# Long convolutions of a hybrid encoder layer: transforms in three rounded passes instead of one fp32 pass, with their matrices streamed in by group

## The chip, the cores and the metric

The kernel runs on one core of one Trainium2 chip. The metric is the device time of one execution in microseconds (us), as the median of the runs shown; smaller is better. The profile was taken of one execution of the same program. Engines are named as in the profile: PE multiplies matrices (PEld loads its weights), DVE is the vector engine, ACT the scalar engine, POOL the GpSimd engine, SP the queue that issues most transfers.

## The reference, cut to what matters

Two sequences of 1024 tokens by 1024 features go through one encoder layer. The layer has a projection, a "hyena" mixer with two long convolutions in a row, a windowed attention, gates, an output projection and a gated feed-forward. The change is in the long convolutions alone:

```python
def bidir_fftconv(u, h_fwd, h_bwd):
    L = u.shape[1]
    k = jnp.concatenate([h_fwd, jnp.zeros_like(h_fwd[:1]), h_bwd[:0:-1]], axis=0)
    k_f = jnp.fft.rfft(k, n=2 * L, axis=0)
    u_f = jnp.fft.rfft(u, n=2 * L, axis=1)
    return jnp.fft.irfft(u_f * k_f[None], n=2 * L, axis=1)[:, :L]

    for o, gate in enumerate((x1, x2)):
        z = gate.astype(jnp.float32) * (bidir_fftconv(z, filt[:, 0, o], filt[:, 1, o])
                                        + hyena_bias[o].astype(jnp.float32) * z)
```

The filters `filt` come from a small network and are the same for both sequences.

## The kernel before

**Products.** Nearly all large products are done in "three rounded passes": an fp32 operand is split into a rounded half `hi` (type fp32r) and the rest `lo`, and hi·hi, hi·lo and lo·hi are accumulated. ACT writes `hi` by a copy that rounds, DVE writes `lo` by a subtraction (`part`, `split`). The transforms of the long convolutions are the exception: they multiply plain fp32 operands.

**Transforms.** A transform of length 2048 is done in eight groups g = 0, 4, 2, 6 (the even half, part 0) and 1, 7, 3, 5 (the odd half, part 1). DVE forms the group's inputs A (128x512) by butterflies (`fwd_butterfly`), and PE multiplies them by a small matrix of the group (`dft`): one product of 512 columns and two of 256, or four of 256 for g = 0. `mats` loads all matrices of a direction once, into a tile of their own for each group, through SP. `conv` takes each group's result X (a PSUM bank of tag `sa`, of which there are two), loads the filter's spectrum K (three buffers), multiplies on DVE (t2, t1, then Y in two halves), transforms back on PE into `sb` or `sc`, and ACT copies the result to B. After the four groups of a half, `inv_even` or `inv_odd` joins them on DVE. The second of the two convolutions (`fm`) takes Y as the weights and the matrix as the moving operand, four products of 256 columns.

**Amount.** `filters` transforms the filters: 2 orders x 2 channel halves x 8 groups = 32 forward transforms. `hyena(s)` does, for each sequence s, 2 channel halves x 2 convolutions x 8 groups: 32 forward and 32 inverse transforms. "A half" below is the four groups between two butterflies, forward and inverse: hyena has eight halves for each sequence.

**Order.** In `main`, a chain of side work (filters, hyena(0), attention(0), hyena(1), attention(1)) is mixed with the projections (the "main" work) at fixed rates: each `yield` tells the cost that is counted. This gives the program's order and priorities. From them the framework fixes, at build time, the order of the instructions on each engine; on the chip every engine runs its list in order and waits where an operand is missing. The main work beside hyena(0) is the gates of sequence 0 (`proj_gates`: DVE scales each product, `ge<-mm,rf`) and then `next_rows`, which splits the normalised rows of sequence 1 (ACT `hh`, DVE `hl`) and starts its projection (`proj_u`); beside hyena(1) it is `proj_qkv` and `proj_gates` of sequence 1, whose results ACT copies out. The weights of the main work come through SP and are split by ACT (`whi`) and DVE (`wlo`).

Of the kernel before, what the change touches and what calls it, by code (L numbers as in the profile page):

```python
# [11 lines left out]
F32 = mybir.dt.float32  # L12
# [30 lines left out]
TB = 3  # L43
PA, YI, KB = 4, 2, 3
AB, YB = 3, 2
RATES = (1.0, 0.85, 1.0, 1.0, 1.1, 1.22, 1.3, 0.3)
# [3 lines left out]
PLACE = {"B11": 0, "B21": 1, "B22": 2, "T1": 3, "T3": 4, "T4": 5, "T2": 6}  # L50
PLAIN = (0, 1, 10)


def shape_constants():
# [30 lines left out]

    c["dft_f"], c["dft_i"], c["dft_f0"], c["dft_i0"] = (np.ascontiguousarray(x.astype(f32)) for x in (fwd, inv, fwd0, inv0))
    bands = 16
# [129 lines left out]
class Kern:  # L217
# [13 lines left out]
    def filters(self):  # L231
        nc, a, tc = self.nc, self.a, self.tc
        self.kd = [[self.dr.tile([P, 8, 3, CH], F32, name=f"kd{o}{h}") for h in range(2)] for o in range(2)]
        with tc.tile_pool(name="fl", bufs=1, side="right", reuse_waits="tile") as pool:
# [34 lines left out]
            with tc.tile_pool(name="fc", bufs=1, side="right", reuse_waits="tile") as cpool:  # L269
                mf = self.mats(cpool, "dft_f")  # L270
                for o in range(2):
# [6 lines left out]
                    for h in range(2):  # L278
# [16 lines left out]
                        for part, op in ((0, ALU.add), (1, ALU.subtract)):  # L295
                            nc.vector.tensor_tensor(sx, kt[:, 0:8], kt[:, 8:16], op)
                            for g, X in self.spectrum(cpool, sx, part, mf):
                                ks = cpool.tile([P, 3, CH], F32, tag="ks", name="ks", bufs=2)
                                nc.scalar.copy(ks[:, 0:2], X)
                                if g == 0:  # L300
                                    nc.scalar.copy(ks[:, 2], X[:, 0])
                                    nc.vector.tensor_copy(ks[0:1, 2], X[0:1, 1])
                                    nc.vector.memset(ks[0:1, 1], 0.0)
                                n = 3 if g == 0 else 2
                                nc.sync.dma_start(self.kd[o][h][:, g, :n], ks[:, :n])
                                yield 3
# [29 lines left out]

    def mats(self, pool, name):

        m = {}
        for g in (0, 4, 2, 6, 1, 7, 3, 5):  # L340
            m[g] = pool.tile([P, 4 if g == 0 else 3, P], F32, tag=f"{name}{g}", name=f"{name}{g}", bufs=1)
            self.nc.sync.dma_start(m[g], self.a[name + "0"][0] if g == 0 else self.a[name][g - 1])
        return m

    def spectrum(self, pool, x, part, mf):
        nc = self.nc
        Ag = {}

        def A(g):
            Ag[g] = pool.tile([P, 2, CH], F32, tag="A", name="A", bufs=AB)  # L350
            return Ag[g]

        def tmp(tag, n):
            return pool.tile([P, n, CH], F32, tag=tag, name=tag, bufs=1)

        for g in fwd_butterfly(nc, x, A, tmp, part):
            X = self.psm().rearrange("p (i c) -> p i c", i=2)
            self.dft(X, mf[g], Ag[g], g)
            yield g, X

    def dft(self, out, m, x, g):
        mm = self.nc.tensor.matmul
        if g:
            mm(out, m[:, 1], x, start=True, stop=False)
            mm(out[:, 0], m[:, 0], x[:, 1], start=False, stop=False)
            mm(out[:, 1], m[:, 2], x[:, 0], start=False, stop=True)
            return
        for o in range(2):
            for i in range(2):
                q = (1, 0, 2, 3)[2 * o + i]  # L370
                self.nc.tensor.matmul(out[:, o], m[:, q], x[:, i], start=(i == 0), stop=(i == 1))

    def conv(self, pool, z, o, h, fm, mf, mi):
        nc = self.nc
# [7 lines left out]
        for part in range(2):  # L382
            cnt = 0
            for g, X in self.spectrum(pool, z, part, mf):
                K = pool.tile([P, 2, CH], F32, tag="K", name="K", bufs=KB)
                nc.sync.dma_start(K, self.kd[o][h][:, g, 0:2])
                Kd = K[:, 0]
                if g == 0:
                    Kd = pool.tile([P, CH], F32, tag="Kd", name="Kd", bufs=1)
                    nc.sync.dma_start(Kd, self.kd[o][h][:, 0, 2])  # L390
                t1 = pool.tile([P, 2, CH], F32, tag="t1", name="t1", bufs=YB)
                t2 = pool.tile([P, 2, CH], F32, tag="t2", name="t2", bufs=1)
                nc.vector.tensor_tensor(t2, X, bc(K[:, 1], 2, 1), ALU.mult)
                if g == 0:
                    nc.vector.tensor_tensor(t1[:, 0], X[:, 0], K[:, 0], ALU.mult)
                    nc.vector.tensor_tensor(t1[:, 1], X[:, 1], Kd, ALU.mult)
                else:
                    nc.vector.tensor_tensor(t1, X, bc(K[:, 0], 2, 1), ALU.mult)
                Y = t1
                nc.vector.tensor_tensor(Y[:, 0], t1[:, 0], t2[:, 1], ALU.subtract)  # L400
                nc.vector.tensor_tensor(Y[:, 1], t2[:, 0], t1[:, 1], ALU.add)
                ps = self.psm("sb" if g % 4 < 2 else "sc")
                B[g] = pool.tile([P, 2, CH], F32, tag="B", name="B", bufs=4)
                if not fm:
                    X2 = ps.rearrange("p (i c) -> p i c", i=2)
                    self.dft(X2, mi[g], Y, g)
                    nc.scalar.copy(B[g], X2)
                else:
                    X2 = ps.rearrange("p (t c) -> p t c", t=2)
                    for t in range(2):  # L410
                        s = slice(P * t, P * t + P)
                        for i in range(2):
                            q = slice(1, 3) if i == 0 else slice(0, 4, 3) if g == 0 else slice(0, 2)
                            nc.tensor.matmul(X2[:, t], Y[:, i, s], mi[g][:, q], start=(i == 0), stop=(i == 1))
                    nc.scalar.copy(B[g].rearrange("p c (t n) -> p t c n", t=2), ps.rearrange("p (t c n) -> p t c n", t=2, c=2))
                cnt += 1
                yield 4.5
# [5 lines left out]
    def hyena(self, s):  # L423
        nc, tc = self.nc, self.tc
        with tc.tile_pool(name="cv", bufs=1, side="right", reuse_waits="tile") as pool:
            mf, mi = self.mats(pool, "dft_f"), self.mats(pool, "dft_i")
            for h in range(2):
# [3 lines left out]
                nc.sync.dma_start(x1, self.x1t[s][:, :, h])  # L431
                for y in self.conv(pool, z, 0, h, False, mf, mi):
                    if isinstance(y, float):
                        yield y
# [3 lines left out]
                yield 2.5  # L438
                for yf in self.conv(pool, y, 1, h, True, mf, mi):
                    if isinstance(yf, float):  # L440
                        yield yf
# [126 lines left out]
    def spread_dma(self, pool, r):  # L568
# [3 lines left out]
        nc.tensor.transpose(pt[:NB, :P], r, self.ident)  # L572
        row = pool.tile([NB, P], F32, tag="row", name="row", bufs=1)
        nc.scalar.copy(row, pt[:NB, :P])
# [857 lines left out]
```

## Time and profile before

| what | value |
|---|---|
| median of 3 runs | 2963.36 us (2956.32 to 2964.63) |
| the profiled execution: its time, its span | 2963.17 us, 2961.4 us |
| filters' transforms | about 148 to 371 us of the span |
| hyena(0) | about 371 to 633 us |
| attention(0) beside the projection of sequence 1 | about 633 to 880 us |
| hyena(1) | about 880 to 1150 us |
| DVE TENSOR_TENSOR of 128x512 | 0.69 us each |
| ACT CAST of 128x512 to fp32r | 0.62 us each |

A row of the grouped view reads: line, engine, operation, out<-in, shape, xcount, then busy time and the mean ns of one, then the idle time before. A row of the timeline reads: start and duration in us, engine, line, operation. A matmul's duration contains the drain of its pipeline, which lies beside the next one; the distance from start to start ("pitch") is what it costs in a row of its kind. The same holds, less strongly, for DVE.

### The profile page before, as it was taken

The numbers are of one execution on the slowest core, as the hardware profiler recorded it, in microseconds if no ns is written. First come the engines' busy times: TensorE is split into PE (matmuls) and PEld (weight loads), VectorE is DVE, ScalarE is ACT, GpSimd is POOL, SyncE is SP. The second block draws the span as 40 slices with busy tenths as digits, with TensorE's granted clock in tenths as the row PEclk, the third lists the DMA queues.
The fourth block names the chain that finished last, engine by engine and source line by source line (L and its number), as shares of the span: only waits on it lengthen the run. The fifth ranks groups of instructions, "written<-read, shape, count | busy, mean of one in ns | idle before, by whom it ended". The sixth has DMA issues, their size and how long they took to land.

```text
span 2961.4 us, 35810 instructions
## 1 busy us (share of the span) xinstructions
PE 2905.0 (98%) x13386; PEld 2349.2 (79%) x13386; DVE 2068.7 (70%) x3361; ACT 1151.4 (39%) x1870; POOL 74.9 (3%) x146
## 2 busy tenths in 40 slices
PE   8999999999999999999999999999999999999998
PEld 6788777778887777777777788888887888888887
DVE  6675698787858755888587667776555767766565
ACT  5322211148841112887464434444111434443122
POOL 0000000000000000000000000000122000001100
PEclk9999999999999999999999999999999999999999
DMA  5444763242253323544776345556666334447641
GB/s 172 143 136 144 263 212 132 100 151 69 77 180 95 141 96 113 159 153 148 221 230 201 121 156 202 205 206 243 262 249 248 136 121 156 157 156 290 260 156 69
DMA packets 202427, 498.29 MB, mean 168 GB/s; under 512 B 19623, under 2 KB 68427, under 8 KB 202253
## 3 DMA queue, kind: packets, MB, share of 16 engines
q1 hardware_dynamic: 182093, 422.60, 41.9%
q0 software_dynamic: 20160, 73.41, 6.3%
q8 instruction: 105, 1.72, 0.2%
q14 instruction: 69, 0.57, 0.1%
HBM read 342.30 MB, written 153.63 MB: 167 GB/s over the span
## 4 chain that ended last, share of the span: by engine, by line
PE 66%; DVE 6%; DMA 4%; ACT 3%; issue 1%; SPq 0%; DVEq 0%; ACTq 0%
PE mm L517 5%; PE mm L518 5%; PE mm L519 5%; PE mm L1003 4%; PE mm L1004 4%; PE mm L1005 4%; PE sa L1003 3%; PE sa L1004 3%; PE sa L1005 3%; PE mm L1200 1%; PE mm L1201 1%; PE mm L1202 1%; PE sb L1003 1%; PE sb L1004 1%; PE sb L1005 1%; PE sc L1003 1%
## 5 line engine op out<-in xcount | busy, mean ns | idle before, releaser
L325 ACT CAST whi<-raw 128x1024 fp32r<-128x1024 f32 (+1 forms) x270 | 264.3, 979 | 627.0 <-PE mm L518 277.6
L326 DVE TENSOR_TENSOR wlo<-raw,whi 128x1024 fp32r<-128x1024 f32 (+1 forms) x270 | 306.3, 1134 | 208.1 <-ACT whi L325 197.7
L518 PE MATMUL mm<-hl,whi 128*128 128x512 f32 x824 | 330.9, 402 | 0.0
L517 PE MATMUL mm<-hh,whi 128*128 128x512 f32 x824 | 330.6, 401 | 0.0
L519 PE MATMUL mm<-hh,wlo 128*128 128x512 f32 x824 | 328.2, 398 | 0.0
L325 ACT CAST whi<-s 128x1024 fp32r<-128x1024 f32 x104 | 109.1, 1049 | 254.8 <-PE mm L1004 57.2
L1003 PE MATMUL mm<-r,whi 128*128 128x512 f32 x528 | 207.9, 394 | 0.2 <-ACT r L325 0.2
L1004 PE MATMUL mm<-r,whi 128*128 128x512 f32 x528 | 206.9, 392 | 0.8 <-DVE r L326 0.8
L1005 PE MATMUL mm<-r,wlo 128*128 128x512 f32 x528 | 206.6, 391 | 0.0
L517 PEld LDWEIGHTS mm<-hh,whi 128*128 128x128 f32 x824 | 155.8, 189 | 30.7 <-issue 0.7
L519 PEld LDWEIGHTS mm<-hh,wlo 128*128 128x128 f32 x824 | 155.6, 189 | 30.4 <-issue 0.5
L518 PEld LDWEIGHTS mm<-hl,whi 128*128 128x128 f32 x824 | 155.8, 189 | 30.2 <-issue 0.5
L1003 PE MATMUL sa<-r,whi 128*128 128x512 f32 x352 | 139.1, 395 | 4.6 <-ACT whi L325 4.6
L1004 PE MATMUL sa<-r,whi 128*128 128x512 f32 x352 | 138.3, 393 | 0.0
L1005 PE MATMUL sa<-r,wlo 128*128 128x512 f32 x352 | 138.2, 393 | 0.0
L326 DVE TENSOR_TENSOR wlo<-s,whi 128x1024 fp32r<-128x1024 f32 x104 | 127.0, 1222 | 13.8 <-ACT whi L325 12.3
L982 POOL DMA_DIRECT2D r<-comb x112 | 59.4, 530 | 2683.9 <-PE mm L1005 2061.1
L1004 PEld LDWEIGHTS mm<-r,whi 128*128 128x128 f32 x528 | 99.1, 188 | 23.1 <-DVE r L326 1.1
L1003 PEld LDWEIGHTS mm<-r,whi 128*128 128x128 f32 x528 | 99.2, 188 | 22.6 <-ACT r L325 0.3
L1005 PEld LDWEIGHTS mm<-r,wlo 128*128 128x128 f32 x528 | 99.1, 188 | 22.7
L725 PE MATMUL mm<-whi,hh 128*128 128x256 f32 x384 | 110.2, 287 | 0.0
L726 PE MATMUL mm<-wlo,hh 128*128 128x256 f32 x384 | 109.3, 285 | 0.0
(471 smaller groups left out, 7036.1 us busy)
## 6 DMA issues: line engine op xcount, KB each, us to landing
r<-comb POOLq DMA_DIRECT2D x112, 512.0 KB, 9.6
comb<-stage SPq DMA_DIRECT2D x48, 1024.0 KB, 5.1
raw<-in_w_fg SPq DMA_DIRECT2D x44, 512.0 KB, 5.6
raw<-in_w_fu SPq DMA_DIRECT2D x44, 512.0 KB, 3.5
raw<-in_w_g SPq DMA_DIRECT2D x32, 512.0 KB, 4.4
gt<-ge SPq DMA_DIRECT2D x32, 512.0 KB, 5.2
K<-kd SPq DMA_DIRECT2D x64, 256.0 KB, 3.5
raw<-in_w_up SPq DMA_DIRECT2D x32, 512.0 KB, 4.4
```

Of the source, the lines that this page charges most:

```text
L325: self.nc.scalar.copy(hi, src)
L326: self.nc.vector.tensor_tensor(lo, src, hi.bitcast(F32), ALU.subtract)
L517: mm(ps, hi[:, k], xh[:, s], start=(i == 0), stop=False)
L518: mm(ps, hi[:, k], xl[:, s], start=False, stop=False)
L519: mm(ps, lo[:, k], xh[:, s], start=False, stop=(i == n - 1))
L725: nc.tensor.matmul(ps[:, q], xh[:, t], wh, start=(i == 0), stop=False)
L726: nc.tensor.matmul(ps[:, q], xh[:, t], wl, start=False, stop=False)
L982: self.nc.gpsimd.dma_start(t.bitcast(F32), src[q][PLACE[name]])
L1003: mm(ps, hi[:, k], xh, start=(first and k == 0), stop=False, skip_group_check=not first)
L1004: mm(ps, hi[:, k], xl, start=False, stop=False, skip_group_check=not first)
L1005: mm(ps, lo[:, k], xh, start=False, stop=(k == n - 1), skip_group_check=not first)
L1200: mm(ps, hi[:, w], xh, start=(first and q == 0), stop=False, skip_group_check=not first)
```

## The change

A transform's matrix is split on the host into `hi` and `lo` (`halves`), and the table holds both. `mat` loads one group's pair when its turn comes, into one of two buffers of that direction, by a transfer that POOL issues and that turns fp32 into fp32r; `mats` is gone. The inputs A and the products Y are split by ACT and DVE (`split`, two buffers each), and each product is done in three passes. To make room, K has two buffers in place of three, A two in place of three, t1 one in place of two, t2 shares the butterfly's `t`, and a small row tile uses another tile's tag.

```diff
-PA, YI, KB = 4, 2, 3
-AB, YB = 3, 2
+PA, YI, KB = 4, 2, 2
+AB, YB = 2, 1
+MB = 2
+def halves(x):
+    x = np.ascontiguousarray(x.astype(np.float32))
+    i = x.view(np.int32)
+    hi = ((i + 0x7FF + ((i >> 12) & 1)) & ~0xFFF).astype(np.int32).view(np.float32)
+    return np.ascontiguousarray(np.stack([hi, x - hi], axis=2))
...
-    c["dft_f"], c["dft_i"], c["dft_f0"], c["dft_i0"] = (np.ascontiguousarray(x.astype(f32)) for x in (fwd, inv, fwd0, inv0))
+    c["dft_f"], c["dft_i"], c["dft_f0"], c["dft_i0"] = (halves(x) for x in (fwd, inv, fwd0, inv0))
...
-    def mats(self, pool, name):
-        m = {}
-        for g in (0, 4, 2, 6, 1, 7, 3, 5):
-            m[g] = pool.tile([P, 4 if g == 0 else 3, P], F32, tag=f"{name}{g}", name=f"{name}{g}", bufs=1)
-            self.nc.sync.dma_start(m[g], self.a[name + "0"][0] if g == 0 else self.a[name][g - 1])
-        return m
+    def mat(self, pool, name, g):
+        src = self.a[name + "0"][0] if g == 0 else self.a[name][g - 1]
+        n = int(np.prod(src.shape[1:]))
+        t = pool.tile([P, 8 * P], F32R, tag=name, name=name, bufs=MB)
+        t = t[:, :n].rearrange("p (e q c) -> p e q c", e=2, q=src.shape[2])
+        self.nc.gpsimd.dma_start(t, src)
+        return t
...
         for g in fwd_butterfly(nc, x, A, tmp, part):
+            m = self.mat(pool, "dft_f", g)
             X = self.psm().rearrange("p (i c) -> p i c", i=2)
-            self.dft(X, mf[g], Ag[g], g)
+            self.dft(X, m, self.split(pool, Ag[g], [P, 2, CH], "A"), g)
             yield g, X
...
+        passes = [(m[:, e], x[f]) for e, f in ((0, 0), (0, 1), (1, 0))]
         if g:
-            mm(out, m[:, 1], x, start=True, stop=False)
-            mm(out[:, 0], m[:, 0], x[:, 1], start=False, stop=False)
-            mm(out[:, 1], m[:, 2], x[:, 0], start=False, stop=True)
+            for n, (w, v) in enumerate(passes):
+                mm(out, w[:, 1], v, start=(n == 0), stop=False)
+            for n, (w, v) in enumerate(passes):
+                mm(out[:, 0], w[:, 0], v[:, 1], start=False, stop=False)
+                mm(out[:, 1], w[:, 2], v[:, 0], start=False, stop=(n == 2))
             return
...
-                t2 = pool.tile([P, 2, CH], F32, tag="t2", name="t2", bufs=1)
+                t2 = tmp("t", 2)
...
+                Y = self.split(pool, Y, [P, 2, CH], "Y")
+                mi = self.mat(pool, "dft_i", g)
...
-                            nc.tensor.matmul(X2[:, t], Y[:, i, s], mi[g][:, q], start=(i == 0), stop=(i == 1))
+                            for n, (e, f) in enumerate(((0, 0), (0, 1), (1, 0))):
+                                nc.tensor.matmul(X2[:, t], Y[f][:, i, s], mi[:, e, q], start=(i == 0 and n == 0), stop=(i == 1 and n == 2))
```

The order shows two places. The first is PE in hyena(0), from the end of the second forward transform of an odd half to the start of the third (`mm` is the gates' product of main work, `hh`, `hl` its moving operands; `Ah`, `Al` the split inputs of the transform). Of the change:

```order
L378 MATMUL sa<-Ah,dft_f 128x256
L379 MATMUL sa<-Ah,dft_f 128x256
L534 MATMUL mm<-hl_306,whi 128x512
L535 MATMUL mm<-hh_305,wlo 128x512
L533 MATMUL mm<-hh_329,whi 128x512
L534 MATMUL mm<-hl_330,whi 128x512
L535 MATMUL mm<-hh_329,wlo 128x512
L533 MATMUL mm<-hh_165,whi 128x512
L534 MATMUL mm<-hl_166,whi 128x512
L535 MATMUL mm<-hh_165,wlo 128x512
L533 MATMUL mm<-hh_185,whi 128x512
L376 MATMUL sa<-Ah,dft_f 128x512
```

Between the second transform and the third stand nine products of main work; the third needs a matrix whose buffer the first one has held.

The second place is DVE in the fifth half of hyena(0) (the first convolution of the second channel half), at the groups 2 and 6. Before:

```order
L393 TENSOR_TENSOR t_3794<-sa,K 128x512
L398 TENSOR_TENSOR t_3793<-sa,K 128x512
L178 TENSOR_TENSOR sd<-t,B 128x512
L400 TENSOR_TENSOR t_3793<-t_3793,t_3794 128x256
L401 TENSOR_TENSOR t_3793<-t_3794,t_3793 128x256
L744 TENSOR_TENSOR ge<-mm,rf 128x512
L393 TENSOR_TENSOR t_3814<-sa,K 128x512
L398 TENSOR_TENSOR t_3813<-sa,K 128x512
```

And of the change, at the same groups (`Yl` and `Al` are the new `lo` halves, `hl` the rows of sequence 1):

```order
L407 TENSOR_TENSOR t<-sa,K 128x512
L342 TENSOR_TENSOR Yl<-t_4496,Yh 128x512
L342 TENSOR_TENSOR Al<-A,Ah 128x512
L412 TENSOR_TENSOR t_4607<-sa,K 128x512
L334 TENSOR_TENSOR hl_5646<-xin,hh_5645 128x512
L414 TENSOR_TENSOR t_4607<-t_4607,t 128x256
L415 TENSOR_TENSOR t_4607<-t,t_4607 128x256
L334 TENSOR_TENSOR hl_5654<-xin,hh_5653 128x512
L407 TENSOR_TENSOR t<-sa,K 128x512
L342 TENSOR_TENSOR Yl<-t_4607,Yh 128x512
L334 TENSOR_TENSOR hl_5654<-xin,hh_5653 128x512
L412 TENSOR_TENSOR t_4651<-sa,K 128x512
```

The `lo` halves stand one instruction behind the value that they split, and the rows of sequence 1 (`hl`), which had come in the last half of hyena(0) and behind it, stand here, three halves ahead of that.

More of the change, by code (lines that the diff above doesn't have):

```diff
@@ L269, in filters @@
             with tc.tile_pool(name="fc", bufs=1, side="right", reuse_waits="tile") as cpool:
-                mf = self.mats(cpool, "dft_f")
                 for o in range(2):
@@ L296, in filters @@
                             nc.vector.tensor_tensor(sx, kt[:, 0:8], kt[:, 8:16], op)
-                            for g, X in self.spectrum(cpool, sx, part, mf):
+                            for g, X in self.spectrum(cpool, sx, part):
                                 ks = cpool.tile([P, 3, CH], F32, tag="ks", name="ks", bufs=2)
@@ L335, in split, with spectrum @@
         return hi, lo
-    def mats(self, pool, name):
-        m = {}
-        for g in (0, 4, 2, 6, 1, 7, 3, 5):
-            m[g] = pool.tile([P, 4 if g == 0 else 3, P], F32, tag=f"{name}{g}", name=f"{name}{g}", bufs=1)
-            self.nc.sync.dma_start(m[g], self.a[name + "0"][0] if g == 0 else self.a[name][g - 1])
-        return m
-    def spectrum(self, pool, x, part, mf):
+    def mat(self, pool, name, g):
[5 more added lines that the diff above has]
+        return t
+    def spectrum(self, pool, x, part):
         nc = self.nc
@@ L370, in dft, with conv @@
                 q = (1, 0, 2, 3)[2 * o + i]
-                self.nc.tensor.matmul(out[:, o], m[:, q], x[:, i], start=(i == 0), stop=(i == 1))
-    def conv(self, pool, z, o, h, fm, mf, mi):
+                for n, (w, v) in enumerate(passes):
+                    mm(out[:, o], w[:, q], v[:, i], start=(i == 0 and n == 0), stop=(i == 1 and n == 2))
+    def conv(self, pool, z, o, h, fm):
         nc = self.nc
@@ L383, in conv @@
             cnt = 0
-            for g, X in self.spectrum(pool, z, part, mf):
+            for g, X in self.spectrum(pool, z, part):
                 K = pool.tile([P, 2, CH], F32, tag="K", name="K", bufs=KB)
@@ L405, in conv @@
                     X2 = ps.rearrange("p (i c) -> p i c", i=2)
-                    self.dft(X2, mi[g], Y, g)
+                    self.dft(X2, mi, Y, g)
                     nc.scalar.copy(B[g], X2)
@@ L425, in hyena @@
         with tc.tile_pool(name="cv", bufs=1, side="right", reuse_waits="tile") as pool:
-            mf, mi = self.mats(pool, "dft_f"), self.mats(pool, "dft_i")
             for h in range(2):
@@ L431, in hyena @@
                 nc.sync.dma_start(x1, self.x1t[s][:, :, h])
-                for y in self.conv(pool, z, 0, h, False, mf, mi):
+                for y in self.conv(pool, z, 0, h, False):
                     if isinstance(y, float):
@@ L438, in hyena @@
                 yield 2.5
-                for yf in self.conv(pool, y, 1, h, True, mf, mi):
+                for yf in self.conv(pool, y, 1, h, True):
                     if isinstance(yf, float):
@@ L572, in spread_dma @@
         nc.tensor.transpose(pt[:NB, :P], r, self.ident)
-        row = pool.tile([NB, P], F32, tag="row", name="row", bufs=1)
+        row = pool.tile([NB, P], F32, tag="t4", name="row")
         nc.scalar.copy(row, pt[:NB, :P])
```

## The prediction

> **What bounds the kernel now.** I read the page's sums, then the engines' busy time by stage, then PE's waits in hyena(0).
>
> ```profile
> span 2961.4 us, 35810 instructions
> PE 66%; DVE 6%; DMA 4%; ACT 3%; issue 1%; SPq 0%; DVEq 0%; ACTq 0%
> 371.00:633.00 262.00, 260.66 (x1084) 201.19 (x1083) 221.55 (x376) 45.35 (x67) 0.00 (x0) 1.00 0.43 145
> 880.00:1150.00 270.00, 269.47 (x1215) 213.16 (x1214) 192.24 (x316) 50.90 (x77) 0.00 (x0) 1.00 0.32 107
> 148.00:371.00 223.00, 216.77 (x1210) 181.47 (x1210) 139.38 (x182) 57.07 (x90) 0.00 (x0) 0.99 0.54 182
> 633.00:880.00 247.00, 244.87 (x1385) 204.28 (x1384) 180.36 (x503) 162.99 (x369) 0.00 (x0) 1.00 0.35 113
> PE tr L705 <- DVE uc L695: 0.8, 1, 0.8
> PE mm L531 <- ACT hh L325: 0.5, 1, 0.5
> ```
>
> The first two lines are the page's span and the chain that ended last: PE holds 66% of it. The next four are stretches: length, then busy time of PE, PEld, DVE, ACT and POOL, the granted clock, the DMA share and GB/s. In hyena(0) (371 to 633) PE is busy 260.66 of 262 us, DVE 221.55, ACT 45.35; in hyena(1) (880 to 1150) DVE has 192.24 of 270. The last two lines are all that PE waited for in hyena(0), 1.3 us. So PE bounds the whole stretch, DVE stands behind it with 40 us of room in hyena(0) and 78 in hyena(1), and ACT has plenty.
>
> **What PE saves.** The groups and the starts of single products:
>
> ```profile
> L364 PE MATMUL sa<-A,dft_f 128*128 128x512 f32 x168 | 87.1, 600 | 1.3 <-ACT ks L299 1.2
> L371 PE MATMUL sa<-A,dft_f 128*128 128x256 f32 x96 | 23.4, 387 | 3.9 <-DVE A L138 2.5 <-issue 1.2
> L414 PE MATMUL sc<-dft_i,t 128*128 128x256 f32 x128 | 31.0, 385 | 0.0
> 528.08 1.02 PE L364 MATMUL sb<-t,dft_i 128*128 128x512 f32 x2
> 529.80 1.02 PE L364 MATMUL sa<-A,dft_f 128*128 128x512 f32 x2
> 609.94 0.39 PE L533 MATMUL mm<-hh,wlo 128*128 128x512 f32 x1
> 614.70 0.39 PE L533 MATMUL mm<-hh,wlo 128*128 128x512 f32 x1
> 187.68 0.28 PE L725 MATMUL mm<-whi,hh 128*128 128x256 f32 x1
> 190.42 0.28 PE L727 MATMUL mm<-whi,hl 128*128 128x256 f32 x1
> ```
>
> The forward group has 168 instructions for 84 products in the code: an fp32 product is two instructions. One transform starts at 528.08, the next at 529.80: 1.72 us for 1024 fp32 columns (one product of 512, two of 256). Rounded products: 21 pitches of 512 columns lie between 609.94 and 614.70, 0.227 us each; 23 of 256 columns between 187.68 and 190.42, 0.119 us each, weight loads included. So a transform in three passes costs 3 x 0.227 + 6 x 0.119 = 1.39 us, or 12 x 0.119 = 1.43 us where it had four products of 256. By the code 112 transforms are of the first kind and 48 of the second (16 of g = 0, 32 of `fm`): 112 x 0.33 + 48 x 0.29 = **50.6 us saved on PE**: 10.3 in the filters, 20 in each hyena.
>
> **What DVE and ACT get.** 160 splits: an ACT copy and a DVE subtraction of 128x512 each.
>
> ```profile
> L325 ACT CAST yh<-yraw 128x512 fp32r<-128x512 f32 x32 | 19.1, 618 | 6.7 <-DMA yraw<-ya 2.8 <-DMA yraw<-yh 1.9 <-PE mm L519 1.5
> 522.41 0.68 DVE L157 SCALAR_TENSOR_TENSOR A<-t,sd 128x512 f32<-128x512 f32 x1
> 523.01 0.68 DVE L159 SCALAR_TENSOR_TENSOR A<-t,sd 128x512 f32<-128x512 f32 x1
> 523.61 1.22 DVE L326 TENSOR_TENSOR wlo<-raw,whi 128x1024 fp32r<-128x1024 f32 x1
> 524.74 0.68 DVE L161 SCALAR_TENSOR_TENSOR sd<-sd,z 128x512 f32<-128x512 f32 x1
> 527.14 0.42 DVE L400 TENSOR_TENSOR t<-t,t 128x256 f32<-128x256 f32 x1
> 527.48 0.42 DVE L401 TENSOR_TENSOR t<-t,t 128x256 f32<-128x256 f32 x1
> L692 DVE SCALAR_TENSOR_TENSOR uc<-mm,sw,uc 128x511 f32<-128x511 f32 x24 | 17.9, 747 | 5.6 <-ACT uc L690 5.4
> 519.61 0.95 DVE L153 TENSOR_TENSOR sd<-z 128x768 f32<-128x768 f32 x1
> L442 DVE TENSOR_TENSOR gx<-gx,y 128x2048 f32<-128x2048 f32 x4 | 9.1, 2287 | 0.1
> DVE sd L180 <- ACT B L407: 5.8, 2, 2.9
> DVE sd L180 <- ACT B L415: 4.9, 2, 2.4
> DVE sd L200 <- ACT B L407: 4.9, 2, 3.2
> DVE sd L200 <- ACT B L415: 5.0, 2, 2.6
> ```
>
> ACT takes 0.62 us each, 64 x 0.62 = 40 us in a hyena on top of 45 or 51: covered by its idle time. On DVE an instruction begins 0.08 us ahead of the end of the one before, so its pitch is 0.60 us for 512 columns (522.41 to 523.01), 1.13 for 1024, 0.34 for 256, and by the same 0.08 0.67, 0.87 and 2.2 for the last forms. A split costs DVE 0.60 us: 38 us in each hyena. Whether that fits is a question for each half. With these pitches I counted the new order, half by half, PE against DVE, and added to DVE the wait for B at the end of a half: the last four rows, 20.6 us in eight halves, 2.6 each. Halves 1 to 4 of hyena(0) come to DVE 31.7 and 38 against PE 31.4 and 39.9 (the even and the odd half), those of hyena(1) to 29.4 and 36.1 against 29.9 and 36.5. There DVE just fits, and PE keeps its gain.
>
> It doesn't in halves 5 to 7 of hyena(0), where the rows of sequence 1 (`hl`) and the first `uc` now stand. DVE: 110 instructions of 512, 46 of 256, 9 of 1024, 2 of 768, 15 of 511, one of 2048 = 66 + 15.6 + 10.2 + 1.7 + 10 + 2.2 = 105.7 us, with three waits for B 113.5. PE: 279 products of 512 (main and transform), 186 of 256 and 28 transposes (some 0.1 each, from the 256-column pitch) = 63.3 + 22.1 + 3 = 88.4. PE waits there for **25 us**, and has nothing else to run, since its list is in order.
>
> In the other halves the pairs cost a little: ACT's `hi` ends 0.62 us and two hand-overs behind its source, one DVE instruction (0.60) stands between, so `lo` waits about 0.2 us. Where DVE just fits, I take 0.4 us for a half, 13 x 0.4 = **5 us**; the bounds are nothing and 13 x 6 x 0.2 = 16. K, with two buffers, is asked for when the product two groups ahead is done, some 3.5 us ahead of its use, against 3.8 us to landing (below): within these 5.
>
> **The tables.** 160 transfers of 384 KB (512 for g = 0) take the place of 40 through SP, now issued by POOL, which has nothing else to do there.
>
> ```profile
> r<-comb POOLq DMA_DIRECT2D x112, 512.0 KB, 9.6
> r<-bs POOLq DMA_DIRECT2D x1, 512.0 KB, 3.5
> K<-kd SPq DMA_DIRECT2D x29, 256.0 KB, 3.8
> ```
>
> The last number is us from issue to landing: the median of POOL's loads in the feed-forward, several in flight; one that started alone; K's median in hyena(0). With two buffers the third table of a half is asked for when the first transform has ended. By the order, the second transform (1.4) and nine main products (2.0) lie between, 3.4 us, while the table needs 3.5 to some 4.4: PE waits 0.1 to 1.0 us. The fourth table and the inverse ones have 4.6 us or more. I take 0.5 us in each of 24 halves, less the three where PE waits for DVE anyhow: **10 us**. No row shows a transfer that also turns fp32 into fp32r. Its price is bounded below by the plain load, nothing added; above I use the 9.6 us, and stay near the row of a load alone. The traffic grows by 64 x 0.4 MB in some 255 us, 100 GB/s on 145 or 107.
>
> The Trainium skill, "DMA: Bandwidth & Descriptors", section "Anatomy of one DMA — SWDGE (gpsimd) path", gives 2.0 us + bytes / 436e3: 2.9 us for such a table and an estimated 3.2 for the load that took 3.5 here; by it the tables would cost nothing and the sum fall by the 10 us. The same page, section "SWDGE vs HWDGE vs iDMA", states that a float32r destination always makes the transfer a cast, which only GpSimd issues; it gives no price, and no run here shows one.
>
> **The sum**, against the profiled execution (2963.17 us, span 2961.4; the median is 2963.36, the same within 0.01%): 2963.2 - 50.6 + 25 + 5 + 10 = **2952.6 us**, 0.36% below. Differences under 0.3% (8.9 us) can't be told from none by a measurement of this kernel.
>
> **The rivals.**
> *All of PE's saving arrives*: the `hl` rows run in DVE's waits and the tables are in time. For it: PE waited 1.3 us in hyena(0). Against: 113 us of DVE over 88 of PE. 2963 - 50.6 + 5 = 2918.
> *The tables come late* (slower). The casting transfer takes over 4.5 us. At 5.5 us the third table is 2.1 us late and the last inverse one, with 4.6 us between its release and use, 0.9: 16 x 3.0 + 8 x 2.1 = 65 in place of 10, so 3008; break-even lies at 4.5 us. For it: 9.6 us when several are in flight, and the added traffic. Against: POOL's queue is otherwise empty.
> *The pairs stop DVE*: `lo` waits for ACT's whole 0.8 us in half of the 128 hyena splits, since ACT's list also holds copies of weights that wait for PE. 64 x 0.6 = 38 in place of 5, so 2986. For it: DVE is above 95% in most halves. Against: ACT is busy less than 40%, and the order puts work between.
> *The change doesn't do what it says*, if rounded passes cost more than their pitch: the qkv rows, with new weights at every product, speak against it; below 2%, counted with the second rival.
>
> **How the numbers follow.** Forecast 40%, from 2935 to 2966 (28 faster, 12 same). All saved 15%. Tables late 27% (24 slower, 3 same). Pairs 18% (7 same, 11 slower). Together faster 0.43, same 0.22, slower 0.35. The range leaves 10% on each side: 2918, where all is saved, to 3020, tables of 5.7 us. The forecast's own range is 2935 to 2966.
>
> **What would show it.** Right: `dft_f` rows at pitches 0.227 and 0.119; PE's waits in hyena(0) named `Yh`, `Al`, `Yl` or `hl`, some 25 us, in its fifth to seventh half; hyena(1) shorter by 15 to 20 us; `dft_f` landing 3.5 to 4.4 us. Wrong: PE waiting for `dft_f` over 1 us in each half, DVE idle behind `Yh` or `Ah` over 3 us in a half, or hyena(1) no shorter.

## The result and the profile after

| | before | changed |
|---|---|---|
| median of 4 runs each | 2963.99 us (2956.32 to 2966.67) | 3047.56 us (3044.85 to 3053.86) |
| ratio, 95% interval | | **1.0296** (1.0279 to 1.0313) |
| span of the profiled execution | 2961.4 us | 3043.6 us |

The change makes the kernel **84 us slower**, where 10.6 us faster was forecast and 3020 was the upper end of the range. The page of the changed kernel, with the sums of busy time and the table loads of 384 KB (the last number is the median of the us from issue to landing):

```profile
span 3043.6 us, 37631 instructions
PE 2900.1 (95%) x13914; PEld 2381.9 (78%) x13914; DVE 2169.2 (71%) x3521; ACT 1240.7 (41%) x2030; POOL 159.5 (5%) x306
dft_f<-in_dft_f POOLq DMA_DIRECT2D x84, 384.0 KB, 4.7
dft_i<-in_dft_i POOLq DMA_DIRECT2D x56, 384.0 KB, 4.2
```

The row of sums from the page of the kernel before:

```profile
PE 2905.0 (98%) x13386; PEld 2349.2 (79%) x13386; DVE 2068.7 (70%) x3361; ACT 1151.4 (39%) x1870; POOL 74.9 (3%) x146
```

PE's idle time rose from 2961.4 - 2905.0 = 56 us to 3043.6 - 2900.1 = 144. Its busy time fell by only 5, though the products are shorter, so something also made PE's work slower: the mean granted clock, in the view of cores of the kernel before and of the changed one, is

```profile
core 0: 2961.4 us, clock 0.992
```

```profile
core 0: 3043.6 us, clock 0.983
```

In both traces the granted clock is either 1 or 0.5 throughout. So PE spent about (1 - 0.983) x 2 x 3043.6 = 103 us at half clock, against 47.

Where it happened, by stage. The borders are the first transform, the first and the last inverse product of each hyena, and the first product of the feed-forward. Each row has the length, then busy time of PE, PEld, DVE, ACT and POOL, granted clock, DMA share, GB/s. Before:

```profile
157.00:374.00 217.00, 211.18 (x1183) 176.56 (x1183) 133.41 (x180) 55.20 (x88) 0.00 (x0) 0.99 0.55 188
374.00:629.00 255.00, 253.66 (x1054) 195.95 (x1053) 215.76 (x365) 44.02 (x65) 0.00 (x0) 1.00 0.44 147
629.00:871.00 242.00, 239.87 (x1366) 201.16 (x1365) 176.14 (x493) 162.57 (x367) 0.00 (x0) 1.00 0.34 109
871.00:1139.00 268.00, 267.47 (x1204) 210.51 (x1202) 189.38 (x315) 50.52 (x76) 0.00 (x0) 1.00 0.34 113
1139.00:1650.00 511.00, 491.38 (x2215) 391.58 (x2213) 377.13 (x751) 307.90 (x583) 0.00 (x0) 0.98 0.55 177
```

And after:

```profile
151.00:443.00 292.00, 250.70 (x1433) 219.08 (x1434) 167.54 (x231) 78.11 (x128) 19.05 (x36) 0.94 0.66 213
443.00:734.00 291.00, 267.29 (x1354) 220.22 (x1353) 256.64 (x439) 89.04 (x143) 30.68 (x58) 0.96 0.62 191
734.00:968.00 234.00, 223.50 (x1343) 192.02 (x1341) 164.79 (x471) 154.84 (x357) 3.17 (x6) 0.97 0.32 101
968.00:1237.00 269.00, 254.43 (x1314) 211.51 (x1315) 228.60 (x375) 85.07 (x136) 30.67 (x58) 0.99 0.64 198
1237.00:1733.00 496.00, 468.06 (x2119) 370.49 (x2117) 374.51 (x749) 302.57 (x577) 0.00 (x0) 0.99 0.56 180
```

The filters take 75 us more, hyena(0) 36 more, hyena(1) 1 more; the stages around hyena(1) are 8 and 15 us shorter (the planner moved some projections forward, so single stages can't be compared to the us). At the feed-forward the kernel is 83 us behind, and behind it nothing changes. The filters, where PE was forecast to save 10 us, lost most: PE is idle for 41 of 292 us, at a clock of 0.94. The stage between the hyenas, with attention(0), is shorter, and yet PE is idle there for 10.5 us at a clock of 0.97, where before it was idle for 2.1 us at full clock; no term of the prediction stood for that.

PE's waits in the changed kernel, in the filters, in hyena(0) and in hyena(1) (engine, line, what was waited for, us in total, times, longest):

```profile
PE sa L376 <- DMA dft_f<-in_dft_f: 24.8, 16, 5.6
PE sa L385 <- ACT Ah L341: 8.2, 4, 4.6
PE sa L293 <- DVE kt L297: 7.8, 7, 2.5
...
PE sa L376 <- DMA dft_f<-in_dft_f: 5.4, 4, 3.1
PE mm L547 <- ACT hh L333: 3.4, 3, 2.5
PE sa L376 <- DVE ge L760: 3.2, 1, 3.2
PE tr L721 <- DVE uc L711: 3.0, 2, 2.0
PE mm L548 <- DVE hl L334: 2.7, 2, 1.8
...
PE sa L376 <- DMA dft_f<-in_dft_f: 8.7, 7, 2.8
PE sc L376 <- DMA dft_i<-in_dft_i: 3.1, 2, 2.0
```

In the filters and in hyena(1) PE waits for tables; in hyena(0) it waits for DVE and ACT, in the names that were forecast (`hl`, `uc`), and less for tables. One row seems to be misnamed: the 3.2 us put down to `ge` end at 553.28, which is 0.13 us behind the landing of a table (issued at 547.02, 6.13 us), the distance that is seen behind the other late tables too. Counted so, tables hold PE in hyena(0) for 9.1 us, and DVE and ACT for 14.5, all of it in its fifth to seventh half. One wait for a table, from the timeline of the filters (start and duration, us; in brackets the idle time before and what ended it):

```profile
294.41 1.72 SPq L614 DMA_DIRECT2D xin<-in_xT  x2
294.91 0.40 PE L376 MATMUL sa<-Al,dft_f 128*128 128x512 f32 x1
295.14 0.40 PE L376 MATMUL sa<-Ah,dft_f 128*128 128x512 f32 x1
295.38 0.28 PE L378 MATMUL sa<-Ah,dft_f 128*128 128x256 f32 x1
295.48 0.53 POOL L351 DMA_DIRECT2D dft_f<-in_dft_f  x1 [42.09 <-PE sa L385]
...
296.65 0.53 POOL L351 DMA_DIRECT2D dft_f<-in_dft_f  x1 [0.64 <-PE mm L743]
...
297.91 0.39 PE L534 MATMUL mm<-hl,whi 128*128 128x512 f32 x1
303.87 0.76 PE L376 MATMUL sa<-Ah,dft_f 128*128 128x512 f32 x1 [5.58 <-DMA dft_f<-in_dft_f]
```

The products run at the forecast pitch (0.23 us for 512 columns). The first two transforms of the half follow one another; when each has ended, POOL asks for the third and the fourth table, at 295.48 and 296.65. PE has 2 us of other products, which are used up at 298.3, and the third table lands at 303.7, 8.3 us after its issue. This is the longest landing of a third table in the trace: two loads of `xin`, 512 KB each, had been issued from 294.41 on.

What such a wait costs beyond itself is seen from another one, here in the timeline:

```profile
199.19 0.38 PE L293 MATMUL sa<-ws1h,hs 128*128 128x256 f32 x1 [1.90 <-DVE kt L297]
```

and in the windows around it, with the columns of the stages:

```profile
196.93:200.34 3.41, 1.51 (x13) 1.31 (x12) 0.69 (x1) 0.53 (x2) 0.00 (x0) 1.00 0.17 60
200.34:203.75 3.41, 3.41 (x18) 3.41 (x17) 0.69 (x1) 0.00 (x0) 0.00 (x0) 0.50 0.22 72
203.75:207.17 3.42, 3.42 (x31) 3.42 (x30) 0.69 (x1) 0.21 (x1) 0.00 (x0) 1.00 0.26 72
```

PE is busy for 1.51 of 3.41 us, and in the 3.41 us behind that the granted clock is 0.50: 18 products pass where 31 pass in the window after. PE's busy time doesn't show it, since a slow product is a busy one. So this wait of 1.9 us cost some 3.6, half of 3.41 more. Each of the 19 stretches at half clock in this trace begins behind a wait; before there were 6. Not every wait has one behind it: PE has 19 waits of 1.9 us or more ahead of 3000 us, 58 us in all; behind four of them the clock stays at 1, and behind the others stand 75 us at half clock, which lose 38.

### The profile page after: what moved, and what is told of

It reads as the page before. It is cut to its first block, busy times and chain, and to the rows that moved or that the text cites. A ratio compares the mean times of both kernels' runs of the same rounds, so it can differ in the third digit from the quotient of the medians.

```text
span 3043.6 us, 37631 instructions
## 1 busy us (share of the span) xinstructions
PE 2900.1 (95%) x13914; PEld 2381.9 (78%) x13914; DVE 2169.2 (71%) x3521; ACT 1240.7 (41%) x2030; POOL 159.5 (5%) x306
## 4 chain that ended last, share of the span: by engine, by line
PE 57%; issue 8%; DMA 6%; DVE 5%; ACT 2%; POOL 1%; DVEq 0%; POOLq 0%; SPq 0%; ACTq 0%
PE mm L1019 4%; PE mm L1020 4%; PE mm L1021 4%; PE mm L533 3%; PE mm L534 3%; PE mm L535 3%; PE sa L1019 3%; PE sa L1020 3%; PE sa L1021 3%; DMA dft_i<-in_dft_i 1%; PE mm L1216 1%; PE mm L1217 1%; PE mm L1218 1%; PE sb L1019 1%; PE sb L1020 1%
## 5 line engine op out<-in xcount | busy, mean ns | idle before, releaser
L376 PE MATMUL sa<-Ah,dft_f 128*128 128x512 f32 x168 | 74.3, 442 | 44.0 <-DMA dft_f<-in_dft_f 38.9
L743 PE MATMUL mm<-whi,hl 128*128 128x256 f32 x384 | 110.6, 288 | 0.0
```

The source lines that it names most:

```text
L376: mm(out, w[:, 1], v, start=(n == 0), stop=False)
L743: nc.tensor.matmul(ps[:, q], xl[:, t], wh, start=False, stop=(i == 7))
```

## The experiments

Two kinds of question: which part of the change costs how much (e1 to e3, e5, e9, e12 to e14), and whether it can be mended (e4, e6 to e8, e10, e11, e15, e16). Every ratio is to the kernel before, run on the same chip.

| run | ratio | 95% interval |
|---|---|---|
| the change | 1.0296 | 1.0279 to 1.0313 |
| e1 tables kept | 1.0020 | 1.0011 to 1.0030 |
| e2 no subtraction | 1.0169 | 1.0145 to 1.0192 |
| e3 neither | 0.9919 | 0.9902 to 0.9935 |
| e4 four buffers in the filters | 1.0194 | 1.0177 to 1.0210 |
| e5 traffic, paced | 1.0178 | 1.0164 to 1.0192 |
| e6 same type | 1.0284 | 1.0266 to 1.0302 |
| e7 filters only | 1.0067 | 1.0054 to 1.0080 |
| e8 three buffers | 1.0117 | 1.0099 to 1.0136 |
| e9 traffic, free | 1.0080 | 1.0065 to 1.0096 |
| e10 subtraction on GpSimd | 1.0411 | 1.0383 to 1.0439 |
| e11 more beside | 1.0238 | 1.0222 to 1.0253 |
| e12 vector work alone | 1.0084 | 1.0068 to 1.0099 |
| e13 no splits | 0.9886 | 0.9868 to 0.9903 |
| e14 small buffers | 1.0019 | 1.0009 to 1.0029 |
| e15 hyena(1) only | 0.9994 | 0.9985 to 1.0003 |
| e16 own row buffer | 0.9986 | 0.9977 to 0.9996 |

**e1 to e4: tables or splits?**

```
 e1   def mat(...):
-        t = pool.tile(..., bufs=MB); gpsimd.dma_start(t, table of g)
+        if len(kept) < MB: kept.append(tile); gpsimd.dma_start(kept[-1], table of g = 0)
+        return kept[g % MB]
 e2   def split(...):
-        lo = pool.tile(...); vector.tensor_tensor(lo, src, hi, subtract)
+        lo = hi
 e3   both
 e4   def mat(...):  bufs=4 if pool.name == "fc" else MB
```

> Each stage loads only two tables of each kind (those of g = 0) and uses them for all groups: the other groups' tables are left out, the products, splits and buffers stay. Theory (late tables, and the half clock behind each long wait): PE's waits for dft_f and dft_i, 44 us in all, go, and with them some 13 stretches of 3.41 us at half clock, 22 us: 3047.6 - 66 = about 2981. Rival 1 (DVE's splits hold PE): the waits turn into waits for Ah, Al, Yh, Yl, and the time stays above 3025. Rival 2 (the rounded products cost more than their pitch): above 3025 too, without waits, at a lower granted clock.

> The subtraction of each split of a transform's input is left out (the rounded half stands for both), so DVE has 160 instructions less, while ACT's copy and PE's three passes stay. Theory (tables hold PE in the filters and in hyena(1), DVE in hyena(0) alone): about 20 us of waits and 12 us of half clock go from hyena(0): about 3015, and the waits for dft_f stay at 35 us or more. Rival 1 (DVE's splits hold PE everywhere): 2960 or less. Rival 2: above 3040.

> Both of the above: no streamed tables and no subtractions (both left out as there). Theory: the two add up, about 2945; all that is left above 2913 (before, less the 50.6 us that the products save) is a changed order. Rival 2 (the rounded products cost more than their pitch): above 2990.

> In the filters dft_f has four buffers in place of two; all else stays. Theory: a table is asked for four transforms ahead, the filters' 25 us of waits for dft_f and some 10 stretches of half clock (17 us) go: about 3007. Rival 3 (the transfers that turn fp32 into fp32r are too slow as a stream, whatever the number of buffers): waits for dft_f in the filters stay above 15 us, and the time above 3030.

Without the stream of tables the time falls by 2.76%, **82 us** of 2962, more than the 66 expected. e1's sums and its row of cores:

```profile
PE 2875.2 (97%) x13914; PEld 2368.9 (80%) x13914; DVE 2168.7 (73%) x3521; ACT 1240.7 (42%) x2030; POOL 80.2 (3%) x156
core 0: 2961.6 us, clock 0.989
```

PE's idle time is 86 us in place of 144, and its busy time 25 less: 65 us at half clock in place of 103 are 19 of these. By stage, with the same products in each, the filters are 46 us shorter and the two hyenas 20 each. The waits did not turn into others, so rival 1 falls for the tables.

Whether it holds for a part is less clear. From e1 to e3, taking the subtractions away gives another 1.01%, 30 us (from the change to e2 1.27%, 38 us; e2 lies near the theory's 3015 and keeps 46 us of waits for `dft_f`). But the edit of e2 and e3 leaves out more than was said: the attention (88 times) and the filters (4 times) call `split` too, so DVE has 252 instructions less and not 160, as the counts of DVE in the sums of e1 and e3 show (3521 and 3269). And most of what PE gains from e1 to e3 lies in the stage with attention(0): its idle time falls from 12 to 4 us there and its half clock from 14 us to none, in hyena(0) from 11 to 5 and from 7 to none. So the 30 us are not the price of the transforms' subtractions alone.

e4 lies 1.02% under the change, 30 us in place of the 40 expected. Of the filters' 24.8 us of waits for tables none is left, so the number of buffers was the limit there; at the first transform of hyena(0) PE now waits 11.2 us for `Ah`, in place of 4.6. Behind that stands DVE, which waits 13.9 us for the load of `z`, where before it waited 0.7: hyena(0) starts late as well, and no run takes this apart.

e3 is 0.8% faster than before, 2935, where the products alone were to give 2913. e3's sums:

```profile
PE 2857.5 (97%) x13914; PEld 2355.4 (80%) x13914; DVE 2015.2 (69%) x3269; ACT 1238.4 (42%) x2030; POOL 80.2 (3%) x156
```

PE's busy time is 47.5 us under that of before. Some 6 of them are half clock that e3 lacks (its clock is 0.994), which leaves 41 of the forecast 50.6. Idle time went the other way: 2931.0 - 2857.5 = 73.5 us against 56.

**e5, e9, e6: lateness, traffic or the change of type?**

```
 e5   use a kept table, load every table into a tile that nothing reads;
+        gpsimd.tensor_copy(d[:, :1], lo[:, 0, :1])     (paces the loads)
 e9   the same without the copy
 e6   -  gpsimd.dma_start(t, src)
      +  gpsimd.dma_start(t, src.bitcast(F32R))
```

> As e1, the products use a table that is loaded once a stage (the other groups' tables are left out), but every transform's load of 384 KB is still made, one at a time, into a buffer that nothing reads, after the transform's input is split. Theory (PE waits for the tables; their traffic alone costs little): within 10 us of e1, 2955 to 2975. Rival (the added traffic slows the other transfers and so everything): above 2990, without a wait for dft_f.

> As e5 (a table that is loaded once a stage is used, the other groups' tables are left out), but the 158 further loads go to a buffer that no instruction reads, and wait for nothing but the load before, so no buffer of the splits is held. They move the same bytes as the changed kernel's. Theory (e5's 48 us came from the instruction that paced the loads and held the buffer of Al): within 10 us of e1's ratio of 1.002, about 2967. Rival (the traffic itself slows the kernel): above 2990.

> The changed kernel, but the tables in memory are declared fp32r, so that the transfer changes no type; order and buffers are the same. Theory (a table is late because two are asked for at once and share the way, whatever the types): the time stays within 8 us of 3047, the median landing of dft_f between 4.3 and 5.0 us. Rival (turning fp32 into fp32r is what makes the transfer slow): landing below 4.0 us, and below 3030.

e5 was a faulty experiment. DVE's waits in it have a row that the change's lack:

```profile
DVE Al L342 <- POOL dft_fd L349: 45.8, 14, 5.9
```

The instruction that paced the loads read `Al` and so held its buffer. e9 leaves it out (its trace has 155 further loads, not 158, and with the kept ones the change's 160) and lies at 1.0080, 0.60% or **18 us** above e1: between the theory and the rival. The traffic costs something, without a wait for a table. Among DVE's waits from 150 to 700 us, those for loads of other data are longer; e9:

```profile
DVE kt L297 <- DMA dcy<-in_decay: 48.6, 18, 4.6
DVE t L407 <- DMA K<-kd: 7.1, 3, 4.5
```

and e1, which has no row for K:

```profile
DVE kt L297 <- DMA dcy<-in_decay: 40.3, 16, 3.8
```

On PE the waits for `kt` rise from 3.7 us in e1 to 11.7 in e9. That leaves 2.96 - 0.80 = 2.16%, **64 us**, for the lateness itself. e9's sums and row of cores:

```profile
PE 2885.4 (97%) x13914; PEld 2376.7 (80%) x13914; DVE 2169.5 (73%) x3521; ACT 1240.9 (42%) x2030; POOL 159.6 (5%) x306
core 0: 2986.5 us, clock 0.984
```

So between e9 and the change PE's idle time grows by 42 us (from 101 to 144). Half clock hardly grows: by its clock e9 has 96 us of it too, behind other waits. e9 sends the loads earlier and denser than the change does, so 18 is the cost of the same bytes, not of the same schedule. e6 is level with the change, with the same order and a median landing of 4.6 us for `dft_f`: declaring the type changes nothing. POOL still issues the transfer in the same way, so this doesn't price a plain copy.

**e8, e11, e10: can it be mended?**

```
 e8   dft_f: tile [P, 2, 3, P], bufs 5 in the filters, 3 in the hyenas; g = 0's fourth matrix in a tile of its own
 e11  e8, and   -  yield 4.5   +  yield 6.0     (conv)
 e10  e8, and   -  nc.vector.tensor_tensor(lo, src, hi, subtract)
                +  nc.gpsimd.tensor_tensor(lo, src, hi, subtract)      (A and Y)
```

> The changed kernel with five buffers for dft_f in the filters and three in the hyenas (the fourth matrix of g = 0 apart, so that a buffer is 384 KB); dft_i keeps two. Theory: e4's gain of 32 us, and the 14 us of the hyenas' waits for dft_f with 5 us of half clock: about 2996. Rival (DVE holds the hyenas, so earlier tables only turn the waits into others): 3010 or more.

> e8, and the convolution hands over 6.0 in place of 4.5 at each yield, so that the planner sets more of the other work beside each group. Theory (a half is too short for DVE and for the tables): hyena(0) and hyena(1) grow longer, and the waits in them shrink by 10 us or more: about 2985. Rival (what is taken from the later stages is missing there): 2997 or more, with waits in the attention.

> e8 (three and five buffers for dft_f), and the 160 subtractions of the transforms' splits go from DVE to GpSimd, whose queue also issues the tables. Theory (DVE holds hyena(0)): DVE loses 96 us, and as in e2 and e3 some 30 us go, to about 2967, if a subtraction of 512 columns takes GpSimd less than 1.2 us. Rival (the subtraction stands behind table loads that wait for their buffer, or GpSimd is slower): PE waits for Al and Yl, 2997 or more.

e8 comes out as expected, 1.79% or 53 us under the change: no wait for `dft_f` is left. What remains above before was not taken apart further; its trace has 5.8 us of waits for `dft_i`, the waits for the splits, among them 10.9 us at the start of hyena(0), and all of the traffic. e11 is worse than e8: PE waits 25.9 us in the attention, where the moved work is missing:

```profile
PE sa L809 <- DVE kv L788: 25.9, 2, 24.3
```

e10 is the slowest of all. GpSimd's groups and PE's first wait (the mean of one is the number behind the busy time, in ns):

```profile
L342 POOL TENSOR_TENSOR Al<-A,Ah 128x512 fp32r<-128x512 f32 x96 | 147.3, 1545 | 409.2 <-ACT Ah L341 408.7
L342 POOL TENSOR_TENSOR Yl<-t,Yh 128x512 fp32r<-128x512 f32 x64 | 82.9, 1295 | 43.3 <-ACT Yh L341 42.8
...
PE sa L385 <- POOL Al L342: 21.3, 21, 5.0
```

By this profile, whose spans of POOL are rough, the subtraction takes 1.3 to 1.5 us, over the 1.2 that the theory allowed, and sits between a transform's input and its second pass.

**e12, e13, e14: DVE's term by itself, and what e3 lacks.**

```
 e12  kernel before, and for A and Y of each transform   +  vector.tensor_tensor(A, A, A, max)
 e13  e3, and A and Y are written as fp32r by DVE; no split
 e14  kernel before:  -  KB = 3; t2 with its own buffer; row with its own buffer
                      +  KB = 2; t2 in the buffer of t; row in that of t4
```

> The kernel before, with fp32 products and resident tables, and one more DVE instruction of 512 columns on each transform's input (a maximum of the tile with itself, in place, which changes no value). Nothing else of the change is there. Theory (DVE has no room for 64 such instructions in hyena(0), little in the filters and hyena(1)): 25 to 35 us slower, about 2990. Rival (PE bounds both hyenas and DVE has room): within 10 us of before.

> As e3 (one set of two tables a stage, no subtractions), and the copies of the 160 splits are left out too: DVE writes the transforms' inputs as fp32r, and that tile stands for both halves. Theory (the products save their 50 us, and the hand-over through ACT costs the rest of the 25): 2912 to 2920. Rival 1 (the products save only about 25): 2930 or more. Rival 2 (the smaller buffers cost it): 2930 or more too, and e14 is then 10 us or more above before.

> The kernel before with the changed kernel's smaller buffers alone: K with two in place of three, t2 in the buffer of t, the row in the buffer of t4. Theory (they cost next to nothing): within 6 us of before. Rival 2: 10 to 25 us slower, with waits for K or t.

e12 has nothing of the change but DVE's 160 instructions and is 0.84% slower, **25 us**. Its hyena(0), from the first inverse product to the last:

```profile
395.00:653.00 258.00, 244.58 (x985) 184.91 (x984) 242.34 (x416) 42.65 (x64) 0.00 (x0) 0.98 0.38 128
```

DVE is busy for 242.3 of 258 us, where before it was 215.8 of 255, and PE is idle for 13.4 us in place of 1.3. So the lack of room on DVE is shown by itself. Of the 25 us, hyena(0) has some 17: 12 more of idle time, and 5 lost in 10 us at half clock (the clock is 0.98 there). In the filters PE is idle for 6 us more.

e13 lies 1.14%, 34 us, under the kernel before, and 0.33% under e3: ACT's copies cost 10 us, give or take 5. The 92 subtractions of the attention and the filters are missing in e13 too, so the products alone give 34 us at the most. Its sums and two of PE's waits:

```profile
PE 2860.1 (98%) x13914; PEld 2359.9 (81%) x13914; DVE 2015.0 (69%) x3269; ACT 1147.4 (39%) x1870; POOL 80.2 (3%) x156
...
PE sa L293 <- DVE kt L297: 6.9, 6, 2.3
...
PE mm L533 <- DVE gin L901: 6.2, 2, 3.4
```

PE's busy time is 44.9 us less than before and its idle time 2929.6 - 2860.1 = 69.5 in place of 56.4. So rival 1 (the products save only 25) falls, and the theory's 2912 to 2920 too: the products give 45 on PE, and 13 come back as waits. e14 explains 6 of these; with the smaller buffers of K, t2 and the row alone (A and t1 stay as before) there is

```profile
PE mm L517 <- DVE gin L885: 7.1, 3, 3.8
```

against 1.2 us before. The last 7 us or so, among them 3 more of waiting for `kt`, stay unexplained.

**e7, e15, e16: three passes only where there is room.** The kernel before with `dft3` (the three passes), `split` and streamed tables in one stage only:

```
 e7   filters:           spectrum(..., None)     four buffers for dft_f
 e15  hyena(1):          mf, mi = None, None     three buffers for dft_f, two for dft_i
 e16  e15, and           -  row in the buffer of t4; Kd with its own buffer
                         +  row with its own buffer; Kd in one of K's
```

> The kernel before, with three rounded passes in the filters alone (four buffers of 384 KB for their tables); both hyenas stay as before. Theory: the filters have DVE to spare and tables in time, so their 10 us of PE arrive less some 3 us of waits: about 2952 to 2955, faster than before. Rival (PE's waits for the split input and kt in the filters take the gain): 2959 or more.

> The kernel before, with three rounded passes in hyena(1) alone (three buffers for dft_f, two for dft_i); filters and hyena(0) keep their fp32 products and resident tables. Theory (DVE has room there, so the 20 us of PE arrive, less the traffic and a few late tables, some 8 us): about 2949, faster than both kernels. Rival (DVE just fits, and late tables and the hand-overs take the 20 us): 2958 or more.

> e15 with the row's own buffer as before; the room comes from Kd, which takes one of K's two buffers in hyena(1). Theory (the shared row buffer cost the 6 us of e14): the wait for gin shrinks below 2 us, and the time to about 2953, ratio 0.997. Rival (K or t, or the mere change of order, costs it): level with before again, ratio 0.999 to 1.001.

e7 is 0.67% slower, 20 us. That is the rival's side, and twice the 10 us of gain that were at stake. No table is waited for; PE waits in the filters for the split input and for `kt` (two of its rows):

```profile
PE sa L293 <- DVE kt L297: 6.2, 5, 2.6
PE sa L399 <- ACT Ah L341: 6.1, 4, 2.5
```

So the filters have time on DVE, but its chain (loads of the decay, `kt`, butterfly, copy, transform) is longer by the copy, and seems to have no slack at the start of a half; no run shortens it. In hyena(1) of e15 PE doesn't wait for the split input, but 5.7 us for tables. e15 is level, as its rival had it, and e16, whose wait for `gin` is 2.7 us (below 2 was expected), lies 0.14% below before (0.04 to 0.23%): faster than both kernels by its interval, but by less than the 0.3% that was set as what can be told, and the theory's 0.3% did not arrive. So there is no version here that clearly beats the kernel before.

## Why the prediction was wrong

By its own terms, in us of a run of 2962:

| term | forecast | measured | by |
|---|---|---|---|
| products in three passes | -50.6 | -34 at the most: -41 to -45 of PE's work, and 13 of new waits, 6 of them from the small buffers | e13, e3, e14 |
| DVE bound in hyena(0) | +25 | +25 in all stages, some 17 of them in hyena(0) | e12 |
| pairs, ACT's copy ahead of `lo` | +5 | +10 (5 to 15) | e3 against e13 |
| tables | +10 | +82: 64 by lateness, 18 by traffic | the change, e9, e1 |
| sum | -10.6 | +83; measured +84 (2.96% are 88) | |

The rows come from runs that differ in more than one thing, so that they add up this well is in part luck.

**Right.** The pitches; most of PE's saving; that ACT has the time; and that DVE stands in the way in the fifth to the seventh half of hyena(0), where all 14.5 us of PE's waits for DVE and ACT lie. Its size is met in part by luck. Half clock, which the forecast didn't count, adds to these waits: 17 us behind them, which lose 8.5. And from the first copy of B in the fifth half to the first in the eighth (600 to 721 us of the changed kernel) DVE is busy for 109 us, near the forecast 105.7, but PE for 106, of which half clock is some 8, where 88 was forecast.

**The step that failed is the tables' term**, "above I use the 9.6 us, and stay near the row of a load alone": 10 us were put there, and the tables cost 82. The mechanism had been named, but the rival didn't have its size either. By its own terms its break-even is 4.3 us and not 4.5 (and 3020 stands for tables of 5.8 us, not 5.7). At the measured median of 4.7 (`dft_f`) they give 33 us. Three things were mis-sized.
*The landing.* In most halves the race of the third table came out about as forecast: over all 24 its median landing is 3.5 us, and PE has 2.9 us of work behind the issue (median); 3.4 were forecast, but POOL issues the load only 0.4 us after the end of the first transform. Six of the 24 landed in 5.2 to 8.3 us, though, and their waits are 20 us. Each of the six had been issued 0.7 to 3.5 us behind a load of 512 or 1024 KB of other work (`xin`, `raw`, `z`, `gx`); that these loads are the cause is read from the trace and not tested. "The fourth table and the inverse ones have 4.6 us or more" did not save them: the fourth, asked for 1.2 us behind the third, landed in 5.3 us (median). The second and fourth tables in the filters cost 11.5 us, the inverse ones 5.3. The row that would have told it was in the prediction: 9.6 us for loads "several in flight".
*The price of a wait.* A us of waiting was counted as a us. The trace of before already had stretches of half clock behind waits (its clock is 0.992, not 1). In the changed kernel tables hold PE for 47 us (with the 3.2 under `ge`), and 34 us at half clock stand behind these waits, which lose 17: together the 64. But e9, without a late table, has nearly as much half clock behind other waits, so this sum is no proof. The rival's price at 5.5 us, 65, meets the lateness only by chance: it had longer waits and no half clock.
*The traffic.* The 100 GB/s more were given with no price. They cost 18 us, by e9, through loads that had been in time by little (`dcy`, K).

**The wrong signs** that the prediction set itself were in fact there: PE waited over 1 us for `dft_f` in the filters' halves (24.8 us in eight), and hyena(1) was no shorter.

## What to carry to other kernels

A resident table that becomes a streamed one needs more buffers than the uses that stand back to back, so that the next load has time to land under the traffic of its stage, not only alone; three and five in place of two gave back 53 of 82 us here. A split that unloads the bounding engine is paid on the next one: count that engine for each stretch of some 30 us, not for the stage. And price a wait of PE of about 2 us or more above its length: in the changed kernel 58 us of such waits lost 38 us more at half clock.

## What the hardware showed that was not expected

- **Half clock behind a partial pause.** PE was busy for 1.51 us of a stretch of 3.41, and the next 3.41 us were granted 0.50. In the change and in the kernel before, the stretches of half clock begin on a grid of 3.413 us. Take the windows of this grid at full clock, from 60 us on: all 22 in which PE was busy for up to 0.45 of the time had half clock behind them, 3 of the 9 from 0.46 to 0.55, and none above that (in e1 and e9 four more, between 0.56 and 0.69, did). The Trainium skill, "TensorE: Matmul & The Clock Gate", section "Part 1: The HAM clock gate (the "warmup" mystery)", gives the same length of window, and says that the clock falls after at least one idle window. The trace disagrees on that: the window was 44% busy, and the wait 1.90 us long.
- **Two table loads issued one after the other**, 1.2 us apart in nearly all halves: over the third and fourth tables of 24 halves the first of the two landed in 3.5 us (median) and the second in 5.3, up to 8.4. A load of 512 KB that started alone in the kernel before had taken 3.5.
- **GpSimd's subtraction of 128x512** took 1.3 to 1.5 us by the profile, DVE's 0.69 (0.60 as a pitch).
